# Low part of the keys on 128 rows instead of 64 in the selected and sliding scores

## The chip, the cores and the metric

One core of one Trainium2 chip runs the whole program. The metric is the device time of one execution in microseconds (us); the median of the runs shown is what counts. The engines are PE (matmul; PEld is its weight load), DVE (vector), ACT (scalar), POOL (GpSimd) and SP (which issues most transfers).

## What is computed

The reference runs a first transformer block with two layers, then a second block. The change lies in the first block's attention, called NSA: 512 tokens, 8 query heads in 2 groups of 4 that share keys and values of 64 channels. Three softmax branches are gated and summed: over compressed keys, over selected key blocks and over a sliding window.

```python
n_slc = T // SLC_BLOCK              # 512 // 64 = 8
top_n = min(SLC_TOPK, n_slc)        # min(16, 8) = 8: every block is selected
...
sc = jnp.einsum('bqhgd,bhqnld->bhgqnl', qc, kg).astype(jnp.float32) * scale
...
sc = jnp.einsum('bqhgd,bkhd->bhgqk', qb, kb).astype(jnp.float32) * scale   # sliding, window 512
p = jax.nn.softmax(jnp.where(mask, sc, NEG_INF), axis=-1)
...
o = g[..., 0:1] * o_cmp + g[..., 1:2] * o_slc + g[..., 2:3] * o_win
```

With 512 tokens, both the selected and the sliding branch are plain causal attention, each with its own keys and values.

## The kernel before

**Products in parts.** A float32 value is held as a high part rounded to the matmul's format (`fp32r`) and a low part, the rest. A gemm takes three passes (high by high, high by low, low by high; lines 223 to 225).

**Where the parts of queries and keys lie.** A head has 64 channels, PE has 128 rows. `qS` holds a head's query with its high part in one half of the rows and its low part in the other; for heads of group 0 the high part is in rows 0 to 63, for group 1 in rows 64 to 127. `khh[kv]` holds the keys' high part of group kv in both halves, for both branches (b = 0 selected, b = 1 sliding). One pass of 128 rows by `khh` so sums two products. The keys' low part lies in `kl`, group 0 in rows 0 to 63 and group 1 in rows 64 to 127; the pass by `kl` takes the 64 rows in which the query's high part is.

**Building the keys.** `nsa_in` projects keys, values and queries. During its last gemm (`gemm_V(512, post_sv, ...)`, the values of another attention) it runs side jobs between weight units. `tr_k(i)` transposes the keys of token tile i (128 tokens): ACT copies the high parts to `khh` (line 901) and half of the compression's input to `KT2` (in `tA`, line 902), DVE subtracts for `kl` (line 905) and copies the other half of `KT2` (line 906). After all four tiles, POOL adds a table to `KT2` (`blocks`, line 929, first for `blk[0]`, then for `blk[1]`), and PE multiplies the sums by the compression's weights (line 938).

**The heads.** `nsa_attn` goes over 32 items per layer: 4 query tiles of 128 rows (i = 0 to 3), 8 heads each. Item t is a pipeline: `s0(t)` scores and exponentials, `s1(t)` scaling, `s2(t)` transposes, `s3(t)` the product with the values, on successive turns of the loop; PE's order is that of the code. For i = 0 the scores of both branches (2 x 128 columns) are one pass by `khh` (line 1084), one by `kl` (line 1085) and two mask passes (line 1087). For i of 1 to 3 each branch has L = 256, 384 or 512 columns, and per branch there is one pass by `khh` (line 1079), one by `kl` (line 1080) and one mask pass of 128 columns with bf16 operands (line 1081). DVE takes the maximum (line 1090), ACT the exponentials (line 1092) into one of four buffers `E[t % 4]`: two of their own, and the gain tiles `gpost` and `gpre`.

**Filling.** Between the steps, `fill` runs pieces of other gemms ("units" of 24 passes of 512 columns, lines 223 to 225). In the heads the units have one PSUM bank, number 7: a unit's first pass waits until ACT has copied the unit before it out. `cmp_turn` (line 1066) uses that bank too.

The borrowed weight slots `K4` hold the key tiles, so profile and order call `khh[0]`, `khh[1]` and `kl` by the slots' names: in the first layer `whi_72`, `wlo_73` and `whi_70`.

Of the kernel before, what the change touches and what calls it, by code (L numbers as in the profile page):

```python
# [8 lines left out]
F32 = mybir.dt.float32  # L9
F32R = mybir.dt.float32r  # L10
# [6 lines left out]
T = 512  # L17
# [156 lines left out]
class Net:  # L174
# [633 lines left out]
    def mix1(self, l):  # L808
        tc = self.tc
        pool = lambda st, name, side: st.enter_context(tc.tile_pool(name=name, bufs=1, side=side))  # L810
        with ExitStack() as st:
            O = pool(st, "oA", "left")
            oA = (O.tile([128, 4, T], F32R, name="oAh"), O.tile([128, 4, T], F32R, name="oAl"))
            tA = O.tile([128, 8, T], F32, name="tA")
            with ExitStack() as sb:
                S = pool(sb, "sv", "right")
                sv = S.tile([128, 4, 512], F32, name="sv")
                with ExitStack() as sn:
                    NP = pool(sn, "nsa", "left")
                    qS = NP.tile([128, 8, T], F32R, name="qS")  # L820
                    vN = NP.tile([128, 4, 2, 128], F32, name="vN")
                    vc = NP.tile([128, 2, 4, 64], F32, name="vc")
                    gt = NP.tile([128, 4, 24], F32, name="gt")
                    gcm = NP.tile([128, 4, 8], F32, name="gcm")
                    with ExitStack() as s2:
                        K4 = self.nsa_in(l, pool(s2, "nsain", "left"), qS, vN, vc, gt, gcm, sv, tA)
                    S = pool(sb, "sqk", "right")
                    sq = S.tile([128, 4, T], F32, name="sq")
                    sk = S.tile([128, 4, T], F32, name="sk")
                    with ExitStack() as s2:  # L830
                        self.nsa_attn(pool(s2, "nsaat", "left"), qS, K4, vN, vc, gt, gcm, oA, sq, sk, tA)
                O = pool(st, "oB", "left")
                oB = (O.tile([128, 4, T], F32R, name="oBh"), O.tile([128, 4, T], F32R, name="oBl"))
                with ExitStack() as s2:
                    self.sb_attn(pool(s2, "sbat", "left"), sq, sk, sv, oB, self.merge_a(oA, tA))
            self.merge_out(st, 4, oB, tA, self.a["g_post_mix"][l], self.a["g_pre_ffn"][l])

    def nsa_in(self, l, R, qS, vN, vc, gt, gcm, sv, tA):
        nc, a = self.nc, self.a
        if not self.begin:  # L840
            self.banks, self.bi = list(range(8)), 0
# [2 lines left out]
        t1 = [self.gpost.rearrange("p (e h s d) -> p e h s d", e=2, h=8, s=2)[:, e] for e in range(2)]  # L844
        t2 = [R.tile([128, 8, 2, 32], F32, name=f"t2_{i}") for i in range(2)]
        KT2 = tA[:, 0:2].rearrange("p a (k n) -> p a k n", k=2)
        blk = [R.tile([128, 16, 2, 31], F32, name="blk"),
               self.gpre[:, 0:992].rearrange("p (l k n) -> p l k n", l=16, k=2)]
        w1 = [R.tile([128, 16, 64], F32, name=f"w1_{i}") for i in range(2)]
        w2 = R.tile([128, 64], F32, name="w2")  # L850
# [3 lines left out]
        half = [slice(0, 64), slice(64, 128)]  # L854
# [37 lines left out]
        def tr_k(i):  # L892
            ps = side_bank()
            v = ps.rearrange("p (k t) -> p k t", k=4)
            for k in range(4):
                nc.tensor.transpose(v[:, k], kr[i][:, k], self.ident)
            tok = slice(i * 128, i * 128 + 128)
            old = [v[h].rearrange("p k (u e) -> p k u e", e=2) for h in half]
            for kv in range(2):
                for h in half:  # L900
                    nc.scalar.activation(khh[kv][h, :, tok], v[half[kv], 2:4], AF.Copy)
                nc.scalar.activation(KT2[half[0], :, kv, i * 64:i * 64 + 64], old[kv][:, 0:2, :, 0], AF.Copy)
            for kv in range(2):
                h = half[kv]
                nc.vector.tensor_sub(kl[h, :, tok], v[h, 2:4], khh[kv][h, :, tok].bitcast(F32))
                nc.vector.tensor_copy(KT2[half[1], :, kv, i * 64:i * 64 + 64], old[kv][:, 0:2, :, 1])

        def tr_q(i):
# [75 lines left out]
        self.gemm_V(280, post_win)  # L984
        K4 = self.W.borrow()
        khh = [t.rearrange("p (b n) -> p b n", b=2) for t in K4[0:2]]
        kl = K4[2].rearrange("p (b n) -> p b n", b=2)
        kc = K4[3][:, 0:896].rearrange("p (c k n) -> p c k n", c=2, k=2)
        nc.vector.memset(kc.bitcast(F32), 0.0)
        gates()  # L990
# [6 lines left out]
            seq(compressed, lambda: tr_q(3))])  # L997
        return K4

    def nsa_attn(self, R, qS, K4, vN, vc, gt, gcm, oA, sq, sk, tA):  # L1000
        nc, PS = self.nc, self.PS
        mm = nc.tensor.matmul
        E = [R.tile([128, 2, T], F32, name=f"E{i}") for i in range(2)]
        E += [t.rearrange("p (b n) -> p b n", b=2) for t in (self.gpost, self.gpre)]
        PT = [h.rearrange("p (b j q) -> p b j q", b=2, j=4)[:, b] for h in self.hn for b in range(2)]
        Ec = tA[:, 6:8].rearrange("p a (i h n) -> p (a i) h n", i=2, h=8)
        khh = [t.rearrange("p (b n) -> p b n", b=2) for t in K4[0:2]]
        kl = K4[2].rearrange("p (b n) -> p b n", b=2)
        kc = K4[3][:, 0:896].rearrange("p (c k n) -> p c k n", c=2, k=2)
        PcT = R.tile([128, 4, 2, 128], F32, name="PcT")  # L1010
        self.banks = [7]
# [9 lines left out]
        sums = [None] * 4  # L1021
# [3 lines left out]
        n = len(items)  # L1025
        Ob = PS[:, 6, :]

        def cmp_scores():
            raw = [E[3].rearrange("p b n -> p (b n)")[:, kv * T:kv * T + T] for kv in range(2)]
            for kv in range(2):  # L1030
                for c in range(2):
                    for g in range(4):
                        mm(PS[:, 4 + kv, :], kc[:, c, kv, 96 - 32 * g:224 - 32 * g], qS[:, 4 * kv + g],
                           start=c + g == 0, stop=c + g == 4)
                if kv:
                    nc.vector.tensor_copy(raw[kv], PS[:, 4 + kv, :])
                else:
                    nc.scalar.activation(raw[kv], PS[:, 4 + kv, :], AF.Copy)
            for kv in range(2):
                ps = PS[:, 4 + kv, :].rearrange("p (i n) -> p i n", i=4)  # L1040
                for i in range(4):
                    nc.tensor.transpose(ps[:, i], raw[kv][:, i * 128:i * 128 + 128], self.ident)
                nc.vector.tensor_add(Ec[:, :, 4 * kv:4 * kv + 4], ps.rearrange("p i (g n) -> p i g n", g=4),
                                     self.cmask[:, :, None, :].to_broadcast([128, 4, 4, 32]))
# [25 lines left out]
        def s0(t):  # L1070
            i, h = items[t]
            kv, g = divmod(h, 4)
            L = (i + 1) * 128
            r = slice(64 * kv, 64 * kv + 64)
            q = qS[:, h, i * 128:L]
            if i:
                S2 = PS[:, 2 * (t % 2):2 * (t % 2) + 2, :L]
                for b in range(2):
                    mm(S2[:, b], q, khh[kv][:, b, :L], start=True, stop=False)
                    mm(S2[:, b], q[r], kl[r, b, :L], start=False, stop=False)  # L1080
                    mm(S2[:, b, i * 128:L], self.identb, self.maskb, start=False, stop=True)  # L1081
            else:
                S2 = PS[:, 2 * (t % 2), 0:256].rearrange("p (b n) -> p b n", b=2)
                mm(S2, q, khh[kv][:, :, :L], start=True, stop=False)
                mm(S2, q[r], kl[r, :, :L], start=False, stop=False)
                for b in range(2):
                    mm(S2[:, b], self.identb, self.maskb, start=False, stop=b == 1)
            e = E[t % 4]
            m, sums[t % 4] = self.sm(2), self.sm(2)
            nc.vector.reduce_max(m, S2, axis=AX.X, negate=True)  # L1090
            for b in range(2):
                nc.scalar.activation(e[:, b, :L], S2[:, b], AF.Exp, bias=m[:, b:b + 1], accum_out=sums[t % 4][:, b:b + 1])

        def s1(t):
            i, h = items[t]
            L = (i + 1) * 128
            e, s = E[t % 4], sums[t % 4]
            nc.vector.reciprocal(s, s)
            nc.vector.tensor_mul(s, s, gt[:, i, h * 3 + 1:h * 3 + 3])
            for b in range(2):  # L1100
                nc.vector.tensor_scalar(e[:, b, :L], e[:, b, :L], s[:, b:b + 1], None, op0=OP.mult)

        def s2(t):
            i, h = items[t]
            e = E[t % 4]
            for b in range(2):
                tb = PS[:, 4 + b, :].rearrange("p (j q) -> p j q", j=4)
                for j in range(i + 1):
                    nc.tensor.transpose(tb[:, j], e[:, b, j * 128:j * 128 + 128], self.ident)  # L1109
                p = PT[2 * (t % 2) + b]  # L1110
                if b:
                    nc.vector.tensor_copy(p[:, :i + 1], tb[:, :i + 1])
                else:
                    nc.scalar.activation(p[:, :i + 1], tb[:, :i + 1], AF.Copy)
# [610 lines left out]
```

## Time and profile before

| | us |
|---|---|
| median of 3 runs (2938.53 to 2940.01) | 2939.97 |
| the profiled execution's own time | 2941.05 |
| its span | 2939.1 |
| PE busy | 2885.7 (98%) |
| DVE busy | 1402.1 (48%) |
| ACT busy | 1130.7 (38%) |
| POOL busy | 369.1 (13%) |

PE is busy nearly throughout, but a matmul's end in the trace is modelled, so a busy PE does not say how fast it goes. What a pass costs is read from the distance between the starts of successive passes. The first layer's heads run from about 110 to 290 us of the span, the second layer's from about 963 to 1143 us.

### The profile page before, as it was taken

Reading aid. Unit: us, or ns where it says so; the run is one execution under the profiler, and the core shown is the slowest. Engines: PE = TensorE matmul, PEld = TensorE weight load, DVE = VectorE, ACT = ScalarE, POOL = GpSimd, SP = SyncE. Lnnn points to the kernel's source line nnn. Section 1 sums busy time; section 2 is a strip of 40 time slices with the busy share of each in tenths; the row PEclk is TensorE's granted clock in tenths of the full one; section 3 lists DMA queues with packets and bytes.
Section 4 is the critical chain, followed back from the end, with each engine's and each line's share of the span. In section 5 each row is a group of like instructions: output and inputs, shape, how many; then the busy total and the mean of one; then the engine's idle time right before and its main releaser. Section 6 shows DMA issues by size and latency. Waiting matters only on the chain.

```text
span 2939.1 us, 34966 instructions
## 1 busy us (share of the span) xinstructions
PE 2885.7 (98%) x14228; PEld 2302.4 (78%) x14228; DVE 1402.1 (48%) x2232; ACT 1130.7 (38%) x2046; POOL 369.1 (13%) x287
## 2 busy tenths in 40 slices
PE   8999999999999999999999999999999999999999
PEld 7777578888878776688888888888776978888887
DVE  4655645544555555555535453233653243533333
ACT  3444644433433445634424342222443232432222
POOL 5221100100122111100101020000522010000000
PEclk9999999999999999999999999999999999999999
DMA  4111023333322111132332323322421222322322
GB/s 157 58 57 30 23 94 111 99 115 96 102 97 88 48 47 32 49 131 72 111 109 91 109 89 97 99 95 95 137 84 52 72 68 98 115 90 89 109 87 79
DMA packets 234322, 255.48 MB, mean 87 GB/s; under 512 B 33073, under 2 KB 193185, under 8 KB 233777
## 3 DMA queue, kind: packets, MB, share of 16 engines
q1 hardware_dynamic: 228016, 233.53, 25.0%
q0 software_dynamic: 4992, 16.94, 1.7%
q10 hardware_dynamic: 1152, 2.77, 0.3%
q8 instruction: 111, 1.82, 0.2%
q14 instruction: 51, 0.41, 0.0%
HBM read 248.60 MB, written 5.53 MB: 86 GB/s over the span
## 4 chain that ended last, share of the span: by engine, by line
PE 91%; DVE 5%; ACT 3%; issue 1%; DMA 0%; DVEq 0%; SPq 0%; ACTq 0%
PE PS L223 25%; PE PS L225 24%; PE PS L224 24%; PE PS L422 2%; PE PS L1189 2%; DVE x L585 1%; PE PS L1123 1%; PE PS L1109 1%; PE PS L1080 1%; PE PS L1484 1%; PE PS L425 1%; PE PS L1223 1%; PE PS L460 1%; PE PS L1213 1%; PE PS L1215 1%
## 5 line engine op out<-in xcount | busy, mean ns | idle before, releaser
L121 DVE TENSOR_TENSOR wlo<-wraw,whi 128x1024 fp32r<-128x1024 f32 (+3 forms) x364 | 437.3, 1206 | 729.2 <-ACT whi L112 729.1
L223 PE MATMUL PS<-Hh,whi 128*128 128x512 f32 x1952 | 777.3, 398 | 1.0 <-ACT PcT L1067 0.6
L225 PE MATMUL PS<-Hh,wlo 128*128 128x512 f32 x1952 | 761.2, 390 | 0.2 <-DVE wlo L121 0.2
L224 PE MATMUL PS<-Hl,whi 128*128 128x512 f32 x1952 | 760.5, 390 | 0.0
L112 ACT ACTIVATE whi<-wraw 128x1024 fp32r<-128x1024 f32 (+2 forms) x432 | 436.8, 1016 | 342.1 <-PE PS L225 286.2
L223 PEld LDWEIGHTS PS<-Hh,whi 128*128 128x128 f32 x1952 | 367.0, 188 | 87.6 <-issue 14.5
L225 PEld LDWEIGHTS PS<-Hh,wlo 128*128 128x128 f32 x1952 | 366.4, 188 | 78.3 <-DVE wlo L121 0.9
L224 PEld LDWEIGHTS PS<-Hl,whi 128*128 128x128 f32 x1952 | 367.0, 188 | 70.1
L121 POOL TENSOR_TENSOR wlo<-wraw,whi 128x1024 fp32r<-128x1024 f32 (+1 forms) x68 | 167.2, 2460 | 1339.1 <-ACT whi L112 1339.1
L223 PE MATMUL PS<-whi,gh 128*128 128x512 f32 x624 | 242.7, 389 | 0.0
L225 PE MATMUL PS<-whi,gl 128*128 128x512 f32 x624 | 242.7, 389 | 0.0
L224 PE MATMUL PS<-wlo,gh 128*128 128x512 f32 x624 | 242.7, 389 | 0.0
L231 ACT ACTIVATE gh<-gg 128x512 fp32r<-128x512 f32 x88 | 55.6, 632 | 327.2 <-DVE gg L643 178.9
L223 PEld LDWEIGHTS PS<-whi,gh 128*128 128x128 f32 x624 | 117.1, 188 | 24.5
L224 PEld LDWEIGHTS PS<-wlo,gh 128*128 128x128 f32 x624 | 117.1, 188 | 24.4
L225 PEld LDWEIGHTS PS<-whi,gl 128*128 128x128 f32 x624 | 117.1, 188 | 24.1
L641 POOL TENSOR_TENSOR gg<-cg,cu 128x512 f32<-128x512 f32 x44 | 56.7, 1289 | 549.4 <-DVE cu L624 549.4
L223 PE MATMUL PS<-whi,Hh 128*128 128x512 f32 (+2 forms) x320 | 118.8, 371 | 2.2 <-ACT whi L112 1.9
L232 DVE TENSOR_TENSOR gl<-gg,gh 128x512 fp32r<-128x512 f32 x88 | 60.9, 692 | 125.7 <-ACT gh L231 125.7
L224 PE MATMUL PS<-wlo,Hh 128*128 128x512 f32 (+2 forms) x320 | 116.8, 365 | 0.5 <-DVE wlo L121 0.5
L225 PE MATMUL PS<-whi,Hl 128*128 128x512 f32 (+2 forms) x320 | 116.3, 363 | 0.4 <-DVE Hl L232 0.4
L1090 DVE TENSOR_REDUCE small<-PS 128x2 f32<-128x256 f32 (+3 forms) x64 | 52.7, 824 | 106.0 <-PE PS L1081 95.0
(341 smaller groups left out, 4140.0 us busy)
## 6 DMA issues: line engine op xcount, KB each, us to landing
wraw<-in_w_in_dram SPq DMA_DIRECT2D x56, 1024.0 KB, 5.0
wraw<-in_w_up_dram SPq DMA_DIRECT2D x40, 1024.0 KB, 5.1
wraw<-in_ffn_w_gate_dram SPq DMA_DIRECT2D x20, 1024.0 KB, 5.2
wraw<-in_ffn_w_up_dram SPq DMA_DIRECT2D x20, 1024.0 KB, 5.2
wraw<-in_w_down_dram SPq DMA_DIRECT2D x16, 1024.0 KB, 5.0
wraw<-in_ffn_w_down_dram SPq DMA_DIRECT2D x16, 1024.0 KB, 5.0
wraw<-in_w_out_dram SPq DMA_DIRECT2D x12, 1024.0 KB, 5.0
wraw<-in_w_down_dram SPq DMA_DIRECT2D x8, 768.0 KB, 4.3
```

Of the source, the lines that this page charges most:

```text
L112: self.nc.scalar.activation(hi, raw, AF.Copy)
L121: self.lo.tensor_sub(lo, raw, hi.bitcast(F32))
L223: mm(out, lh, rh, start=start, stop=False)
L224: mm(out, lh, rl, start=False, stop=False)
L225: mm(out, ll, rh, start=False, stop=stop)
L231: nc.scalar.activation(hi, src, AF.Copy)
L232: nc.vector.tensor_sub(lo, src, hi.bitcast(F32))
L422: self.nc.tensor.matmul(ps[:, sl], ww[:, k], self.Hh[:, k, sl], start=k == 0 and ww is w[0], stop=False)
L425: self.nc.tensor.matmul(ps[:, sl], w[0][:, kk], self.Hl[:, kk, sl], start=False, stop=kk == 7)
L641: nc.gpsimd.tensor_mul(g, cg[j % 3], cu[j % 3])
L1090: nc.vector.reduce_max(m, S2, axis=AX.X, negate=True)
L1189: mm(z, sk[r, p, j * 128:j * 128 + 128], sq[r, p, j * 128:], start=True, stop=False)
```

## The change

There is a second tile for the keys' low part, `kl1`, so that `kll[0]` and `kll[1]` hold the low part of group 0 and 1 in both halves of the rows. The pass by the low part then takes all 128 rows of `qS`, which adds the product of the two low parts. In blocks of i from 1 to 3 the masks of both branches come after the four score passes. `tr_k` subtracts twice per group instead of once. For the room, the exponentials use three buffers instead of four (`E[t % 3]`), the compressed scores are copied through `PcT` instead of `E[3]`, and `blk[0]` lies in `tA[:, 2:4]`, which is free at that time.

```diff
+                    kl1 = NP.tile([128, 1024], F32R, name="kl1")
...
-        blk = [R.tile([128, 16, 2, 31], F32, name="blk"),
+        blk = [tA[:, 2:4].rearrange("p a n -> p (a n)")[:, 0:992].rearrange("p (l k n) -> p l k n", l=16, k=2),
...
             for kv in range(2):
-                h = half[kv]
-                nc.vector.tensor_sub(kl[h, :, tok], v[h, 2:4], khh[kv][h, :, tok].bitcast(F32))
+                for h in half:
+                    nc.vector.tensor_sub(kll[kv][h, :, tok], v[half[kv], 2:4], khh[kv][half[kv], :, tok].bitcast(F32))
...
+        kll = [t.rearrange("p (b n) -> p b n", b=2) for t in (K4[2], kl1)]
...
-        E = [R.tile([128, 2, T], F32, name=f"E{i}") for i in range(2)]
+        E = [R.tile([128, 2, T], F32, name="E0")]
...
-            raw = [E[3].rearrange("p b n -> p (b n)")[:, kv * T:kv * T + T] for kv in range(2)]
+            raw = [PcT.rearrange("p i k q -> p (i k q)")[:, kv * T:kv * T + T] for kv in range(2)]
...
-            r = slice(64 * kv, 64 * kv + 64)
...
                 for b in range(2):
-                    mm(S2[:, b], q, khh[kv][:, b, :L], start=True, stop=False)
-                    mm(S2[:, b], q[r], kl[r, b, :L], start=False, stop=False)
+                    for k in (khh[kv], kll[kv]):
+                        mm(S2[:, b], q, k[:, b, :L], start=k is khh[kv], stop=False)
+                for b in range(2):
                     mm(S2[:, b, i * 128:L], self.identb, self.maskb, start=False, stop=True)
...
-                mm(S2, q, khh[kv][:, :, :L], start=True, stop=False)
-                mm(S2, q[r], kl[r, :, :L], start=False, stop=False)
+                for k in (khh[kv], kll[kv]):
+                    mm(S2, q, k[:, :, :L], start=k is khh[kv], stop=False)
...
-            e = E[t % 4]
+            e = E[t % 3]
```

On PE, a block of i = 1 in the first layer between two fill units, before (`identb` and `maskb` are the mask's operands):

```order
L225 MATMUL PS<-Hh,wlo_67 128x512
L1079 MATMUL PS<-wlo_73,qS 128x256
L1080 MATMUL PS<-whi_70,qS 128x256
L1081 LDWEIGHTS identb
L1081 MATMUL PS<-maskb,identb 128x128
L1079 MATMUL PS<-wlo_73,qS 128x256
L1080 MATMUL PS<-whi_70,qS 128x256
L1081 LDWEIGHTS identb
L1081 MATMUL PS<-maskb,identb 128x128
L223 MATMUL PS<-Hh,whi_66 128x512
```

and now (`kl_154` is the new tile):

```order
L225 MATMUL PS<-Hh,wlo_67 128x512
L1080 MATMUL PS<-wlo_73,qS 128x256
L1080 MATMUL PS<-kl_154,qS 128x256
L1080 MATMUL PS<-wlo_73,qS 128x256
L1080 MATMUL PS<-kl_154,qS 128x256
L1082 LDWEIGHTS identb
L1082 MATMUL PS<-maskb,identb 128x128
L1082 LDWEIGHTS identb
L1082 MATMUL PS<-maskb,identb 128x128
L223 MATMUL PS<-Hh,whi_66 128x512
```

The eight passes stay eight; the first mask pass has moved behind the second branch's score passes, and the passes by the low part name another tile.

On DVE, the last token tile of `tr_k` in the first layer and the row after it, before:

```order
L905 TENSOR_TENSOR whi_70<-PS,whi_72 64x2x128
L906 COPY tA<-PS 64x2x64
L905 TENSOR_TENSOR whi_70<-PS,wlo_73 64x2x128
L906 COPY tA<-PS 64x2x64
L121 TENSOR_TENSOR wlo_69<-wraw_65,whi_68 128x1024
```

and now:

```order
L906 TENSOR_TENSOR whi_70<-PS,whi_72 64x2x128 x2
L907 COPY tA<-PS 64x2x64
L906 TENSOR_TENSOR kl_154<-PS,wlo_73 64x2x128 x2
L907 COPY tA<-PS 64x2x64
L121 TENSOR_TENSOR wlo_69<-wraw_65,whi_68 128x1024
```

Each group's one subtraction has become two, so the last copy to `tA` (which is `KT2`) stands behind two more instructions of its tile. PE, DVE and ACT otherwise keep their order in these places; POOL and SP keep theirs throughout.

## Rows read from the trace of the kernel before

**Rows 1.** The page: chain that ended last, share of the span by engine.

```profile
PE 91%; DVE 5%; ACT 3%; issue 1%; DMA 0%; DVEq 0%; SPq 0%; ACTq 0%
```

**Rows 2.** Busy time of engines in one stretch of the heads (PE, PEld, DVE, ACT, POOL).

```profile
148.00:190.00 42.00, 41.28 (x242) 30.48 (x241) 22.11 (x52) 17.42 (x56) 9.63 (x4) 1.00 0.16 51
```

**Rows 3.** Waits of PE, first layer's heads: total, times, longest.

```profile
PE PS L1066 <- ACT PcT L1067: 0.4, 1, 0.4
PE PS L1123 <- ACT hn L1114: 0.4, 1, 0.4
PE PS L1084 <- DVE qS L918: 0.2, 1, 0.2
```

**Rows 4.** Timeline of PE, a block of 256 columns: start, duration, engine, line.

```profile
155.72 0.28 PE L1079 MATMUL PS<-wlo,qS 128*128 128x256 f32 x1
155.92 0.38 PE L1080 MATMUL PS<-whi,qS 64*128 64x256 f32 x1
156.24 0.23 PE L1081 MATMUL PS<-maskb,identb 128*128 128x128 bf16 x1
156.27 0.36 PE L1079 MATMUL PS<-wlo,qS 128*128 128x256 f32 x1
156.57 0.38 PE L1080 MATMUL PS<-whi,qS 64*128 64x256 f32 x1
156.88 0.23 PE L1081 MATMUL PS<-maskb,identb 128*128 128x128 bf16 x1
156.92 0.47 PE L223 MATMUL PS<-Hh,whi 128*128 128x512 f32 x1
```

**Rows 5.** Timeline of PE: ten passes of 512 columns, then a 512-column block.

```profile
278.10 0.40 PE L225 MATMUL PS<-Hh,wlo 128*128 128x512 f32 x1
...
280.16 0.39 PE L225 MATMUL PS<-Hh,wlo 128*128 128x512 f32 x1
280.39 0.39 PE L1079 MATMUL PS<-wlo,qS 128*128 128x512 f32 x1
...
282.04 0.47 PE L223 MATMUL PS<-Hh,whi 128*128 128x512 f32 x1
```

**Rows 6.** Timeline of PE: seventeen passes of 280 columns, first and last.

```profile
74.23 0.29 PE L223 MATMUL PS<-whi,Hh 128*128 128x280 f32 x1
...
76.28 0.29 PE L224 MATMUL PS<-wlo,Hh 128*128 128x280 f32 x1
```

**Rows 7.** Timeline of PE, a block of the first query tile.

```profile
115.80 0.38 PE L1085 MATMUL PS<-whi,qS 64*128 64x256 f32 x1
116.12 0.28 PE L1087 MATMUL PS<-maskb,identb 128*128 128x128 bf16 x2
116.21 0.47 PE L223 MATMUL PS<-Hh,whi 128*128 128x512 f32 x1
```

**Rows 8.** Timelines of ACT and PE at one fill unit's end.

```profile
158.79 0.59 ACT L1015 ACTIVATE sq<-PS 128x512 f32<-128x512 f32 x1
159.81 0.48 PE L223 MATMUL PS<-Hh,whi 128*128 128x512 f32 x1
```

**Rows 9.** Timeline of DVE: last token tile of the key transposes.

```profile
92.20 0.42 DVE L905 TENSOR_TENSOR whi<-PS,whi 64x256 fp32r<-64x256 f32 x1 [0.78 <-ACT tA L902]
...
93.28 0.29 DVE L906 COPY tA<-PS 64x128 f32<-64x128 f32 x1
```

**Rows 10.** Timeline of POOL: the first add ahead of the compression.

```profile
93.70 3.43 POOL L929 TENSOR_TENSOR blk<-tA,pe 128x992 f32<-128x992 f32 x1 [14.98 <-ACT whi L112]
```

**Rows 11.** Waits of PE in the gemm ahead of the heads.

```profile
PE PS L938 <- POOL gpre L929: 2.0, 1, 2.0
PE PS L938 <- POOL blk L929: 1.1, 1, 1.1
```

**Rows 12.** Stretches after those waits, two layers: busy times, PEclk, DMA share, GB/s.

```profile
101.00:104.00 3.00, 3.00 (x31) 2.69 (x28) 0.00 (x0) 1.65 (x3) 0.00 (x0) 0.50 0.00 0
951.00:957.00 6.00, 5.36 (x68) 5.07 (x69) 1.67 (x1) 1.62 (x3) 0.59 (x1) 0.50 0.05 16
```

More of the change, by code (lines that the diff above doesn't have):

```diff
@@ L824, in mix1 @@
                     gcm = NP.tile([128, 4, 8], F32, name="gcm")
+                    kl1 = NP.tile([128, 1024], F32R, name="kl1")
                     with ExitStack() as s2:
-                        K4 = self.nsa_in(l, pool(s2, "nsain", "left"), qS, vN, vc, gt, gcm, sv, tA)
+                        K4 = self.nsa_in(l, pool(s2, "nsain", "left"), qS, vN, vc, gt, gcm, kl1, sv, tA)
                     S = pool(sb, "sqk", "right")
@@ L830, in mix1 @@
                     with ExitStack() as s2:
-                        self.nsa_attn(pool(s2, "nsaat", "left"), qS, K4, vN, vc, gt, gcm, oA, sq, sk, tA)
+                        self.nsa_attn(pool(s2, "nsaat", "left"), qS, K4, vN, vc, gt, gcm, kl1, oA, sq, sk, tA)
                 O = pool(st, "oB", "left")
@@ L836, in mix1, with nsa_in @@
             self.merge_out(st, 4, oB, tA, self.a["g_post_mix"][l], self.a["g_pre_ffn"][l])
-    def nsa_in(self, l, R, qS, vN, vc, gt, gcm, sv, tA):
+    def nsa_in(self, l, R, qS, vN, vc, gt, gcm, kl1, sv, tA):
         nc, a = self.nc, self.a
@@ L986, in nsa_in @@
         khh = [t.rearrange("p (b n) -> p b n", b=2) for t in K4[0:2]]
-        kl = K4[2].rearrange("p (b n) -> p b n", b=2)
+        kll = [t.rearrange("p (b n) -> p b n", b=2) for t in (K4[2], kl1)]
         kc = K4[3][:, 0:896].rearrange("p (c k n) -> p c k n", c=2, k=2)
@@ L998, in nsa_in, with nsa_attn @@
         return K4
-    def nsa_attn(self, R, qS, K4, vN, vc, gt, gcm, oA, sq, sk, tA):
+    def nsa_attn(self, R, qS, K4, vN, vc, gt, gcm, kl1, oA, sq, sk, tA):
         nc, PS = self.nc, self.PS
         mm = nc.tensor.matmul
-        E = [R.tile([128, 2, T], F32, name=f"E{i}") for i in range(2)]
+        E = [R.tile([128, 2, T], F32, name="E0")]
         E += [t.rearrange("p (b n) -> p b n", b=2) for t in (self.gpost, self.gpre)]
@@ L1007, in nsa_attn @@
         khh = [t.rearrange("p (b n) -> p b n", b=2) for t in K4[0:2]]
-        kl = K4[2].rearrange("p (b n) -> p b n", b=2)
+        kll = [t.rearrange("p (b n) -> p b n", b=2) for t in (K4[2], kl1)]
         kc = K4[3][:, 0:896].rearrange("p (c k n) -> p c k n", c=2, k=2)
@@ L1096, in s1 @@
             L = (i + 1) * 128
-            e, s = E[t % 4], sums[t % 4]
+            e, s = E[t % 3], sums[t % 4]
             nc.vector.reciprocal(s, s)
@@ L1104, in s2 @@
             i, h = items[t]
-            e = E[t % 4]
+            e = E[t % 3]
             for b in range(2):
```

## The prediction

> **What bounds the kernel now.** I read the chain that ended last first: 91% of it is PE [rows 1]. In the heads, where the scores are, a stretch of 42 us shows PE busy for 41.28, DVE for 22.11 and ACT for 17.42 [rows 2]. The list of PE's waits over the first layer's heads holds five entries, 1.7 us in all, of which three matter here [rows 3]. So a pass that PE gets through sooner moves the end, unless one of those few waits, or a new one, swallows it. A "busy" PE hides the price of a pass, since matmul ends are modelled. The timeline of starts shows it, and there the passes on 64 rows stand out.
>
> **What the 64-row passes cost.** Take a block of 256 columns [rows 4]. From the pass by `khh` to the pass by `kl` it takes 0.20 us (155.72 to 155.92), from there to the mask 0.32, to the next `khh` pass 0.03, then 0.30, 0.31 and 0.04: 1.20 us from the first pass to the next gemm's first. Passes that stay on 128 rows go far quicker: ten of 512 columns have nine distances in 2.06 us, 0.229 each [rows 5], and seventeen of 280 columns have sixteen in 2.05 us, 0.128 each [rows 6]. Every one of these has its own weight load. The slope between them, 0.101 us over 232 columns, gives 0.118 us for 256 columns and 0.173 for 384, an estimate by that line. Each step onto and off 64 rows therefore adds about 0.08 and 0.20 us to what the columns take: PE evidently doesn't hide the new weights behind the running pass when the number of rows changes, and the way back costs more.
>
> **The change, part by part.**
>
> *Blocks of i = 1 to 3.* Now: four passes on 128 rows at the steady distance and two masks. Two masks in a row up to the next pass are seen in a block of the first tile: 116.12 to 116.21, 0.09 us [rows 7]. So 256 columns take 4 x 0.118 + 0.09 = 0.56 us instead of 1.20, saving 0.64. A 512-column block takes 1.65 us now (280.39 to 282.04) [rows 5] and then 4 x 0.229 + 0.09 = 1.01, saving 0.64. For 384 columns the middle of 1.20 and 1.65 is 1.43, against 4 x 0.173 + 0.09 = 0.78: again 0.64. With 8 heads, 3 tiles and 2 layers there are 48 blocks: 30.7 us.
>
> *Blocks of i = 0.* The step from `khh` to the low part goes from 0.20 (taken from [rows 4], same shape) to 0.118, that from the low part to the mask from 0.32 (115.80 to 116.12) [rows 7] to 0.118: 0.28 us each, 16 blocks, 4.5 us. Gross, that is 35.2 us.
>
> *What waits give back in the heads, per layer.* In i = 0 I count five of eight blocks as lost. After block 0 the next block waits for DVE's part of the queries (0.2 us, line 1084), and after block 4 the value product waits for an ACT copy (0.4 us, line 1123) [rows 3]; both ends hang on other engines. After blocks 3, 5 and 7 PE needs bank 7, and ACT's copy ends only 0.05 to 0.07 us before PE takes the bank. That is 5 x 0.28 = 1.4 us. The first block of i = 1 runs ahead of the second `cmp_turn`, which waits for `PcT` (0.4 us) [rows 3]; only the 0.28 us by which block 7 lets that copy start sooner remain, so 0.36 is lost. In i = 1 to 3 the bank is handed over at 11 unit ends. At the tightest one, ACT's copy runs 158.79 to 159.38 and PE takes the bank at 159.81 [rows 8], 0.43 us later; less 0.05 for the signal, 0.38 of that block's 0.64 are free and 0.26 are lost. Five others have 0.64 or 0.65 us and lose about 0.04 each, the remaining five have 0.69 to 3.7 and lose nothing: 0.45 us with the first. Sum 2.2 us, for two layers 4.4. Net 30.8 us.
>
> *Building the second low part.* DVE does four more instructions per group and layer, 0.42 us each. A token tile takes DVE 1.37 us now (92.20 to 93.28 + 0.29), after 0.78 us of waiting for ACT [rows 9]: ACT sets a period of 2.15 us. With two more subtractions DVE needs 1.37 + 0.84 = 2.21. The idle time covers the first three tiles but for 0.06 each; the last copy to `KT2` comes 0.84 + 3 x 0.06, about 1.0 us later. Behind it stand POOL's add, which starts at 93.70, just after DVE's last copy (93.57) [rows 10], and PE, which already waits 1.1 and 2.0 us for POOL there [rows 11]. So this lands on PE in full: 1.0 us a layer, 2.0 us. Without a delay of DVE it would be nothing; that bounds it below. Above, PE's idle time there is followed by a low clock: 3 us at granted clock 0.50 in the first layer, 6 in the second (1.2 GHz instead of 2.4) [rows 12]. If a longer idle time brings 3 us more of it per layer, half of that is lost, 3 us for both; if less, up to 1.5 us per layer come back.
>
> *Three buffers instead of four, `PcT` for the raw scores, `blk[0]` in `tA`.* Nothing. Item t takes the buffer of t-3, whose transposes stand ahead of `s0(t)` in PE's own order, and the exponential waits for that block's scores anyhow. `PcT` is written by `cmp_turn` only after six items; the gate units write `tA[:, 2:4]` long after the compression. The cover would be gone only if an exponential could precede its scores.
>
> *Sum.* 30.8 - 2.0 = 28.8 us. The profiled execution took 2941.05 us (span 2939.1), so 2912.2 for one like it; it lies 1.1 above the median of 2939.97, and from that I forecast 2911.2 us.
>
> **A rule that speaks against it.** The distances on 128 rows leave hardly any room for an exposed weight load: 0.128 us for 280 columns [rows 6]. The Trainium skill, TensorE: Matmul & The Clock Gate, Part 3 (What overlaps and what doesn't), says that a weight load overlaps a running matmul only where the row groups differ. By that, two passes on the same 128 rows should expose it, and this trace disagrees. The sum by that rule stands among the rivals.
>
> **The rivals.**
>
> *The way back belongs to the mask.* In this block the 0.20 us between the low part and the mask follow a change of rows and also one of format, fp32r to bf16; no row shows the second alone. If the format is the cause, one of two stays per block: 0.64 - 0.20 = 0.44 for 48 blocks, 21.1 us, and 0.08 for 16, 1.3 us; less waits (0.8 us a layer, the bank being hardly touched) and 2.0 for DVE: 18.8 us, so 2921.2. For it: nothing but that both coincide; against it, the change onto 64 rows costs without a change of format.
>
> *Weight loads stay exposed.* The first step's 0.20 us (0.31 at 512 columns by the slope) then holds for all four passes: 4 x 0.20 + 0.09 = 0.89 and 4 x 0.31 + 0.09 = 1.33, saving 0.31 and 0.32; 48 blocks 15.1 us, 16 of 0.12 us 1.9, less 1.6 and 2.0: 13.4 us, so 2926.6. Against it [rows 5, 6].
>
> *Bank 7 takes it.* Were each of the 22 handovers in i = 1 to 3 to cost a whole block's saving, 14.1 us would go, of which 0.9 are counted: 2924.4. Against it is the room measured at the other handovers.
>
> *It doesn't do what it says.* If the slow steps came from loading the same query tile twice, they would stay, and only DVE's 2.0 us be added: 2942. Against it: gemm passes too repeat their weights (lines 223 and 224 in a fill unit differ only in one operand) at 0.229.
>
> *Slower.* PE's longer idle time ahead of the compression keeps the clock at 0.50 [rows 12] beyond the few us seen. It decides from 29 us of PE work per layer at that clock (half of 58 is the whole gain), and past 0.2% slower from 35. Lasting through the first two query tiles, some 80 us a layer, it would cost 40 each: 2991. For it only that the second layer shows twice the first's low stretch; against it, PE is dense after it and the clock comes back within 7 us in both.
>
> **How the numbers follow.** My forecast 0.76, the mask 0.12, exposed loads 0.05, bank 7 0.03, no effect 0.02, slower 0.02. The likeliest gives 2911.2. Downwards, the bound is that nothing is given back and DVE's part is hidden: 2939.97 - 35.2 = 2904.8, and 1.5 for a shorter low clock: 2903. Upwards the range takes in the mask's case, 2921.5, which leaves about 0.12 out. 0.2%, 5.9 us, is about what a measurement of this kernel can tell from no change. Faster by more: 0.96, the first four cases; within: 0.02; slower: 0.02.
>
> **What would show it.** In the changed profile, the distances inside a 256-column block should be 0.12, 0.12, 0.12, 0.12 and 0.09; a distance of 0.3 ahead of the first mask shows the mask's case, 0.20 between score passes exposed loads. PE's waits should show bank 7 (line 223 for ACT `sq`, `sk` or `tA`) with a few tenths, and line 939 for POOL with 1.0 us more in each layer. The heads of each layer should be shorter by 15.4 us, and nothing else should move. The forecast is wrong if the blocks shrink but the heads don't, or if PEclk stays at 0.5 for long after the compression.

## The result and the profile after

The changed kernel takes 2909.62 us (median of 4 runs, 2909.34 to 2910.56); the kernel before, run beside it, 2939.25 (4 runs, 2937.72 to 2940.01). The ratio is 0.99, with a 95% interval of 0.9887 to 0.9912: 29.6 us less. The forecast was 2911.2 in a range of 2903.0 to 2921.5. The profiled execution after took 2909.57 us with a span of 2907.6, against 2939.1 before: 31.5 us less. (The profiled execution of before lay 1.8 above the median measured beside the change; that is the difference between 31.5 and 29.6.)

On the page of after, PE's busy time has gone from 2885.7 to 2852.1 us, 33.6 less, and DVE's has risen by 16.3. The chain that ended last is still PE's (compare [rows 1]):

```profile
PE 2852.1 (98%) x14228; PEld 2301.0 (79%) x14228; DVE 1418.4 (49%) x2248; ACT 1130.1 (39%) x2046; POOL 370.0 (13%) x287
...
PE 92%; DVE 4%; ACT 2%; issue 1%; DMA 0%; DVEq 0%; ACTq 0%; POOL 0%; POOLq 0%
```

**The block.** PE's timeline of after, the same 256-column block as in [rows 4]; columns are start, duration, engine, line, operands:

```profile
155.46 0.28 PE L1080 MATMUL PS<-wlo,qS 128*128 128x256 f32 x1
155.57 0.28 PE L1080 MATMUL PS<-kl,qS 128*128 128x256 f32 x1
155.69 0.28 PE L1080 MATMUL PS<-wlo,qS 128*128 128x256 f32 x1
155.81 0.28 PE L1080 MATMUL PS<-kl,qS 128*128 128x256 f32 x1
155.93 0.29 PE L1082 MATMUL PS<-maskb,identb 128*128 128x128 bf16 x2
156.03 0.48 PE L223 MATMUL PS<-Hh,whi 128*128 128x512 f32 x1
```

The distances between starts are 0.11, 0.12, 0.12, 0.12 and, for the two masks, 0.10: 0.57 us, where it was 1.20. At 512 columns the block takes 1.01 us (255.33 to 256.34), where it was 1.65 [rows 5].

**The waits.** PE's waits in the first layer's heads after (engine and line, releaser, total, times, longest):

```profile
PE PS L1067 <- ACT PcT L1068: 1.0, 1, 1.0
PE PS L1043 <- DVE PcT L1037: 0.4, 1, 0.4
PE PS L1110 <- ACT hn L1115: 0.3, 1, 0.3
PE PS L1086 <- DVE qS L919: 0.2, 1, 0.2
```

Against [rows 3]: the second `cmp_turn` now waits 1.0 instead of 0.4, and the wait of the value product for ACT's `hn` (line 1123 before, 1124 now) is gone. Ahead of the heads the two waits for POOL are 1.6 and 2.0, where [rows 11] has 1.1 and 2.0:

```profile
PE PS L939 <- POOL gpre L930: 2.0, 1, 2.0
PE PS L939 <- POOL tA L930: 1.6, 1, 1.6
```

**Where the time came from**, by the starts of the same steps in both traces:

| step | forecast, us | measured, first / second layer |
|---|---|---|
| up to the key transposes (`tr_k`) | 0 | +0.50 / +0.24 |
| `tr_k` to the first compression matmul | +1.0 | +0.78 / +0.78 |
| compression to the first scores | 0 | +0.97 / -1.04 |
| heads | -15.4 | -16.48 / -16.51 |
| of which i = 0 | -0.84 | -1.96 in the first layer |
| of which i = 1 to 3 | -14.55 | -4.56, -4.82, -5.13 = -14.52 (rounded) in the first layer |
| behind the second layer's heads | 0 | -0.74 |

The forecast's shares of the heads follow from its own terms: 8 x 0.28 - 1.4 for i = 0, and 24 x 0.64 - 0.36 - 0.45 for the rest.

### The profile page after: what moved, and what is told of

Read it like the earlier page. It is cut to its first block, busy times and chain, and to the rows that moved or that the text cites. A ratio compares the mean times of both kernels' runs of the same rounds, so it can differ in the third digit from the quotient of the medians.

```text
span 2907.6 us, 34978 instructions
## 1 busy us (share of the span) xinstructions
PE 2852.1 (98%) x14228; PEld 2301.0 (79%) x14228; DVE 1418.4 (49%) x2248; ACT 1130.1 (39%) x2046; POOL 370.0 (13%) x287
## 4 chain that ended last, share of the span: by engine, by line
PE 92%; DVE 4%; ACT 2%; issue 1%; DMA 0%; DVEq 0%; ACTq 0%; POOL 0%; POOLq 0%
PE PS L223 26%; PE PS L225 25%; PE PS L224 25%; PE PS L422 2%; PE PS L1190 2%; DVE x L585 1%; PE PS L1124 1%; PE PS L1110 1%; PE PS L1485 1%; PE PS L1080 1%; PE PS L425 1%; PE PS L460 1%; PE PS L1224 1%; PE PS L1214 1%; PE PS L1216 1%; DVE hn L339 1%
```

## The experiments

The theory: changing the number of rows between passes costs time on PE, about 0.08 us on and 0.20 off, whatever the formats; filling the rows removes it. Rivals: the cost belongs to the mask's format, to the 64-row pass itself, or to another part of the change (its order, its three buffers). A second question came from the waits for POOL: what the second low part costs, and whether that can be had back. Lines in the rows are those of each experiment's own file.

**Rows alone.** The changed kernel with everything as changed (two tiles, masks last, three buffers), but the low pass on 64 rows:

```diff
-                    for k in (khh[kv], kll[kv]):
-                        mm(S2[:, b], q, k[:, b, :L], start=k is khh[kv], stop=False)
+                    mm(S2[:, b], q, khh[kv][:, b, :L], start=True, stop=False)
+                    mm(S2[:, b], q[r], kll[kv][r, b, :L], start=False, stop=False)
...
-                for k in (khh[kv], kll[kv]):
-                    mm(S2, q, k[:, :, :L], start=k is khh[kv], stop=False)
+                mm(S2, q, khh[kv][:, :, :L], start=True, stop=False)
+                mm(S2, q[r], kll[kv][r, :, :L], start=False, stop=False)
```

> The changed kernel with one thing undone: the pass by the low part takes 64 rows again (second tile, masks at the end, three buffers all stay). Theory, that the change of the number of rows is what costs: a 256-column block takes 0.20 + 0.31 + 0.20 + 0.31 + 0.09 = 1.1 us or more again, of which the 0.31 from a 64-row pass to the next khh pass has no change of format, so the way back costs without the mask; time 2937 to 2942 us. Rival, that the masks' place or the buffers brought the gain: 2910 to 2925 us.

2944.52 us (10 runs) against 2940.34 for before beside it (13 runs): ratio 1.0014, interval 1.0004 to 1.0023. The whole gain is gone. PE's timeline of this kernel, a block of 256 columns:

```profile
156.54 0.28 PE L1080 MATMUL PS<-wlo,qS 128*128 128x256 f32 x1
156.75 0.38 PE L1081 MATMUL PS<-kl,qS 64*128 64x256 f32 x1
157.06 0.39 PE L1080 MATMUL PS<-wlo,qS 128*128 128x256 f32 x1
157.38 0.38 PE L1081 MATMUL PS<-kl,qS 64*128 64x256 f32 x1
157.69 0.28 PE L1083 MATMUL PS<-maskb,identb 128*128 128x128 bf16 x2
157.78 0.47 PE L223 MATMUL PS<-Hh,whi 128*128 128x512 f32 x1
```

The third row is the one to read: 156.75 to 157.06 is 0.31 us from 64 rows to 128 with no mask and no change of format. In the changed kernel the step from the low part to the mask, with a change of format and of weights (from the query tile to `identb`) and without one of rows, takes 0.12. So the 0.20 us belong to the rows, and the mask's rival falls, and with it the thought that new weights cost as such. That the kernel lies 2.5 us above the highest time expected is the rest of the change without its gain: a block takes 1.24 us instead of 1.20, the heads are 0.99 and 0.95 us longer than before, the added subtractions cost some 0.8 per layer, together 3.5 of the 4.2 us.

**Grouped passes.** Before, with nothing but the order changed: both high passes, both low ones on 64 rows, both masks.

```diff
                 for b in range(2):
                     mm(S2[:, b], q, khh[kv][:, b, :L], start=True, stop=False)
+                for b in range(2):
                     mm(S2[:, b], q[r], kl[r, b, :L], start=False, stop=False)
+                for b in range(2):
                     mm(S2[:, b, i * 128:L], self.identb, self.maskb, start=False, stop=True)
```

> The kernel before with the passes of a block in another order: khh, khh, low, low (on 64 rows as before), mask, mask; no second tile. Theory, that each CHANGE of the number of rows costs: 256 columns take 0.12 + 0.20 + 0.12 + 0.31 + 0.09 = 0.84 instead of 1.20 us, 48 blocks save 17 us, less about 2 for waits: 2922 to 2927 us. Rival, that each PASS on 64 rows is slow in itself: the distance between the two low passes is 0.2 to 0.3 us, a block about 1.0, time 2930 to 2935 us.

2924.25 us (4 runs), ratio 0.9947, interval 0.9932 to 0.9961: 16.1 us less, with the same passes on the same rows. Timeline of PE (x2 is two passes in one row):

```profile
153.40 0.40 PE L1079 MATMUL PS<-wlo,qS 128*128 128x256 f32 x2
153.73 0.50 PE L1081 MATMUL PS<-whi,qS 64*128 64x256 f32 x2
154.16 0.28 PE L1083 MATMUL PS<-maskb,identb 128*128 128x128 bf16 x2
154.25 0.47 PE L223 MATMUL PS<-Hh,whi 128*128 128x512 f32 x1
```

From the first low pass to the mask it takes 0.43 us, which is one steady distance of 0.12 and one way back of 0.31. A 64-row pass behind another costs what a 128-row pass does; the change of rows is what costs. The block takes 0.85 us. One change in and out per block instead of two is worth 0.35 of the 0.64, and 48 x 0.35 = 16.8 is what came: the heads are 8.43 and 8.44 us shorter in the two layers.

**Three buffers alone.** Before with `E[t % 3]`, `raw` in `PcT` and one `E` tile less:

```diff
-        E = [R.tile([128, 2, T], F32, name=f"E{i}") for i in range(2)]
+        E = [R.tile([128, 2, T], F32, name="E0")]
...
-            e = E[t % 4]
+            e = E[t % 3]
```

> The kernel before with three exponential buffers instead of four and the compressed scores copied through PcT, nothing else. Theory, that these cost nothing because PE's own order already keeps a buffer free: the distances and PE's waits in the heads are those of before, and the time is that of before within 2 us. Rival, that a buffer less holds up an exponential and so a later step: waits of ACT on PE's transposes and a longer stretch of heads, 2942 us or more.

2940.27 us (10 runs) against 2940.39 (19 runs): ratio 0.9998, interval 0.9988 to 1.0007. The heads agree with before within 0.03 us. Nothing, as the prediction had it. (The place of `blk[0]` was not tried by itself.)

**The wait that vanished.** In i = 0 the gain was 1.1 us larger than forecast, all of it between the fifth block and the sixth. PE's timeline of before there shows the product with the values standing for 1.41 us (135.19 to 136.60); in the changed kernel the same eight matmuls take 0.59. Before:

```profile
135.19 0.43 PE L1123 MATMUL PS<-hn,vN 128*64 128x128 f32 x2
136.01 0.65 PE L1123 MATMUL PS<-hn,vN 128*64 128x128 f32 x6 [0.39 <-ACT hn L1114]
136.60 0.44 PE L1109 MATMUL PS<-cf,gpost 128*128 128x128 f32 x2
```

And after:

```profile
136.58 0.66 PE L1124 MATMUL PS<-hn,vN 128*64 128x128 f32 x8
137.17 0.44 PE L1110 MATMUL PS<-cf,gpre 128*128 128x128 f32 x2
```

ACT's copy `hn` was late because ACT waited 2.97 us for DVE's addition to the compressed scores. Timeline of ACT, then those of DVE and POOL, before:

```profile
134.74 1.06 ACT L1052 ACTIVATE tA<-tA 128x1024 f32<-128x1024 f32 x1 [2.97 <-DVE tA L1051]
135.70 0.26 ACT L1114 ACTIVATE hn<-PS 128x128 f32<-128x128 f32 x1
```

```profile
131.29 3.41 DVE L1051 TENSOR_TENSOR tA<-tA,small 128x1024 f32<-128x1024 f32 x1
...
131.14 2.48 POOL L121 TENSOR_TENSOR wlo<-wraw,whi 128x1024 fp32r<-128x1024 f32 x1 [9.24 <-ACT whi L112]
```

And after:

```profile
132.66 1.22 DVE L1052 TENSOR_TENSOR tA<-tA,small 128x1024 f32<-128x1024 f32 x1
...
132.80 3.34 POOL L121 TENSOR_TENSOR wlo<-wraw,whi 128x1024 fp32r<-128x1024 f32 x1 [8.94 <-ACT whi L112]
```

Before, POOL's subtraction began 0.15 us ahead of DVE's addition, and DVE took 3.41 us; now DVE begins 0.14 us ahead, takes 1.22, and POOL takes 3.34 instead of 2.48. Whoever comes second ends about its own time after the other (DVE 1.08 us behind POOL's end, POOL 2.26 behind DVE's). The Trainium skill, SBUF — State Buffer (SBUF: two separate sides), says that a GpSimd operation and a DVE operation with two inputs in SBUF take turns at a shared pair of ports, whole instruction by whole instruction; these rows agree.

Every trace of this case has it the same way, in both layers: the addition takes 3.41 or 3.42 us in the five kernels with the low part on 64 rows and POOL at work (before, rows alone, grouped, three buffers, before with the copies first), and 1.22 in the changed kernel and all variants of it on 128 rows. As the rows-alone kernel, which has the rest of the change, keeps 3.42, it is the low pass on 128 rows that turned the meeting. In the changed kernel the next DVE operation of this size meets POOL instead (3.39 us, 0.08 behind POOL's start), but no wait of PE is listed for it.

To test that the wait hangs on this meeting, before had its low parts in the heads made on DVE, so that POOL is not there at all:

```diff
-        self.W.defer, self.W.lo = True, nc.gpsimd
+        self.W.defer = True
```

> The kernel before, the low parts of the fill units' weights in the heads made by DVE instead of POOL. Theory, that the wait of the value product for ACT's copy (0.4 us, line 1123, the fifth item) comes from a DVE addition that takes 3.41 us beside a POOL subtraction instead of 1.2: that addition takes 1.2 us, the wait goes, and the stretch from the first to the ninth item is shorter by up to 0.8 us in each layer. Rival, that the wait has another source: it stays at 0.4 us.

One run, 2944.42 us. DVE's addition in it:

```profile
132.97 1.22 DVE L1051 TENSOR_TENSOR tA<-tA,small 128x1024 f32<-128x1024 f32 x1
```

The wait for `hn` is gone from the list of PE's waits, and the stretch up to the sixth block is shorter by 0.42 and 0.49 us in the two layers, about half of the 0.8 hoped for. The addition is short again but begins 1.68 us later, behind DVE's own subtraction; so it ends 0.51 sooner, `hn` starts 0.52 sooner (135.18), and the product takes 0.98 us (135.10 to 136.08). The heads as a whole are 2.87 and 1.25 us slower, for DVE now has POOL's work: in the first layer PE waits 1.3 us for ACT's `PcT` copy later on. That POOL's subtraction stretches the addition, and that the wait hangs on the addition's end, is shown; the full 0.8 us is not reproduced by this edit.

**What the second low part costs.** Five kernels reorder DVE's (and ACT's) work of `tr_k`, so that the copies to `KT2`, for which POOL and then PE wait, come sooner. The plainest, from the changed kernel, puts both copies of a tile ahead of its four subtractions:

```diff
             for kv in range(2):
+                nc.vector.tensor_copy(KT2[half[1], :, kv, i * 64:i * 64 + 64], old[kv][:, 0:2, :, 1])
+            for kv in range(2):
                 for h in half:
                     nc.vector.tensor_sub(kll[kv][h, :, tok], v[half[kv], 2:4], khh[kv][half[kv], :, tok].bitcast(F32))
-                nc.vector.tensor_copy(KT2[half[1], :, kv, i * 64:i * 64 + 64], old[kv][:, 0:2, :, 1])
```

> The changed kernel, DVE's two copies to KT2 put ahead of its four subtractions within each token tile. Theory, that the added subtractions delay POOL's add by way of the last copy: PE's first wait for POOL ahead of the compression goes from 1.6 to 0.6 us or less in each layer, 2906 to 2909 us. Rival, that the longer wait came from something else (POOL, ACT): both waits stay at 1.6 and 2.0 us and the time at 2909.6.

2903.51 us (4 runs), ratio 0.9876, interval 0.9859 to 0.9892: 2.5 us below the least expected. PE's waits ahead of the heads:

```profile
PE PS L940 <- POOL gpre L931: 2.5, 1, 2.5
PE PS L914 <- DVE kl L908: 0.4, 1, 0.4
```

2.9 us instead of 3.6. That alone is 1.4 us over two layers. The rest is clock, from the windows (length, busy times, then PEclk). After, first layer, then second:

```profile
100.80:102.00 1.20, 1.20 (x24) 1.20 (x26) 0.99 (x1) 0.00 (x0) 0.00 (x0) 0.50 0.01 2
102.00:106.00 4.00, 4.00 (x50) 3.79 (x49) 0.00 (x0) 1.51 (x2) 0.00 (x0) 0.50 0.01 4
...
938.50:940.00 1.50, 1.50 (x40) 1.50 (x42) 0.98 (x1) 0.00 (x0) 0.00 (x0) 0.74 0.00 1
940.00:943.00 3.00, 3.00 (x35) 2.81 (x32) 0.00 (x0) 1.44 (x2) 0.00 (x0) 0.56 0.00 0
```

With the copies first:

```profile
97.00:100.00 3.00, 0.51 (x13) 0.37 (x13) 2.91 (x5) 2.34 (x2) 2.61 (x1) 1.00 0.46 118
100.00:104.00 4.00, 4.00 (x70) 3.60 (x67) 1.48 (x2) 2.19 (x3) 0.00 (x0) 1.00 0.51 178
...
934.00:940.00 6.00, 6.00 (x46) 5.08 (x42) 1.75 (x3) 2.78 (x4) 0.00 (x0) 1.00 0.12 42
```

After loses half of 5.2 us in the first layer, 2.6, and 0.26 x 1.5 + 0.44 x 3 = 1.7 in the second; here PE comes out of its idle time at the full 2.4 GHz. 1.4 and 4.3 make 5.7 of the 6.1 us between the two medians; by the starts, from `tr_k` to the first scores, it is 3.3 and 2.3 us in the two layers.

The same kernel was run once more, on another chip, beside the changed one, also run again.

> The changed kernel as it is, timed beside the next one on the same chip: 2908 to 2912 us.

> The changed kernel with DVE's copies first in each token tile, as run before (2903.5 us), now beside the changed kernel: 2902 to 2906 us, and its profile shows again no fall of the clock in the first layer. Rival, that the gain over the changed kernel beyond about 2 us was the chance of where the low clock fell: 2906 to 2909 us.

The changed kernel: 2909.39 us, ratio 0.9891, interval 0.9874 to 0.9907. The copies first: 2907.5 (2902.09, 2907.11, 2907.9 and 2909.41), ratio 0.9883, interval 0.9868 to 0.9898, which misses what was expected and lies in the rival's range. But the rival's place is not the right one: the waits are the same to a tenth, and PEclk is 1.00 at this place again in its profiled run of 2907.11. That run and the first one's profiled run (2904.24) keep step within 0.4 us at each step of the table above, up to the end of the second layer's heads; in the 12 us behind them the second loses 3.0 us, at granted clock 0.50 (1.2 GHz). The same window in the first run, then in the second:

```profile
1112.00:1118.00 6.00, 6.00 (x29) 3.50 (x28) 4.01 (x11) 3.77 (x10) 0.00 (x0) 1.00 0.00 0
...
1112.00:1118.00 6.00, 6.00 (x18) 3.50 (x17) 2.77 (x8) 3.37 (x9) 0.00 (x0) 0.50 0.00 0
```

The kernel is the same, and so is the idle time of 0.84 us just ahead in both. Of the 6.1 us by which this order beat the changed kernel at first, 1.9 are left beside it; what the copies first are worth for certain is the shorter waits.

The mirror of it in the kernel before (both copies ahead of the two subtractions):

> The kernel before, DVE's two copies to KT2 ahead of its two subtractions in each token tile. Theory, that most of what this order brought the changed kernel is PE's wait ahead of the compression and the low clock behind it, which stand in the kernel before too: the waits of 1.1 and 2.0 us shrink by about 0.4, and 0 to 2 us per layer of low clock go: 2935 to 2939 us. Rival, that it only repairs what the added subtractions cost: the time of before within 1 us.

2936.91 us (10 runs), ratio 0.9991, interval 0.9981 to 1.0, in the range expected, though the interval reaches 1: PE's waits for POOL fall from 1.1 and 2.0 to one of 2.4. From `tr_k` to the first scores it takes 0.71 and 1.69 us less in the two layers; the clock fell in both all the same (mean PEclk 0.76 from 99 to 106 us and from 949 to 956). The start of the first layer's heads moved by -0.01 us and that of the second by -3.13, but +0.70 and -1.46 of that came ahead of `tr_k`, where nothing was changed.

Moving the subtractions further back was tried in two ways. First, all copies of the four tiles ahead of all high parts and subtractions, which stand in `tr_k2`:

```diff
-            seq(*[lambda i=i: tr_k(i) for i in range(4)]),
+            seq(*[lambda i=i: tr_k(i) for i in range(4)], *[lambda i=i: tr_k2(i) for i in range(4)]),
...
```

> The changed kernel, all copies to KT2 (ACT's and DVE's, four token tiles) ahead of all high parts and subtractions. Theory, that PE's waits of 1.6 and 2.0 us ahead of the compression hang on the time of the last copy alone: POOL's adds end before PE comes to them, both waits go, 3.6 us a layer, and the low clock behind them shrinks (up to 2 us a layer): 2898 to 2903 us. Rival, that the high and low parts, now later, hold up the weights' low parts or the first scores: waits on lines 224 or of the first score pass appear, 2906 to 2910 us.

2908.72 us (4 runs), ratio 0.9894, interval 0.9879 to 0.9908. The rival came true. POOL starts at 89.56 instead of 95.03, PE no longer waits for it, but the PSUM banks of the key transposes are read out later, and the query transposes need them:

```profile
PE PS L919 <- DVE kl L913: 3.2, 2, 2.2
```

Second, ACT's and DVE's copies first in each tile, and the subtractions one tile later:

```diff
+                nc.vector.tensor_copy(KT2[half[1], :, kv, i * 64:i * 64 + 64], old[kv][:, 0:2, :, 1])
...
+            for i2 in ([i - 1] if i else []) + ([i] if i == 3 else []):
+                tok2 = slice(i2 * 128, i2 * 128 + 128)
...
+                        nc.vector.tensor_sub(kll[kv][h, :, tok2], trk[i2][half[kv], 2:4], khh[kv][half[kv], :, tok2].bitcast(F32))
```

> The changed kernel, the copies to KT2 of a token tile ahead of its high parts on ACT, and on DVE ahead of the subtractions of the tile before. Theory: POOL's first add starts about 2.7 us sooner than with the copies first in each tile on DVE alone, PE's wait of 2.5 us ahead of the compression falls below 0.6 in each layer, the clock does not fall there, and no long wait for the transposes' banks appears: 2897 to 2901 us. Rival, that PE then waits for those banks as it did with all copies first: 2904 to 2909 us.

2905.7 us (4 runs), ratio 0.9883, interval 0.9869 to 0.9898: the rival again, in the first layer 3.1 us of waits at the query transposes. DVE's timeline shows what was not foreseen, that each of DVE's copies waits for ACT's copy of the same group:

```profile
88.64 0.28 DVE L904 COPY tA<-PS 64x128 f32<-64x128 f32 x1 [1.92 <-ACT tA L903]
89.26 0.29 DVE L904 COPY tA<-PS 64x128 f32<-64x128 f32 x1 [0.34 <-ACT tA L903]
```

POOL's first add so started at 95.29, no sooner than in the changed kernel.

From the two misses: copies first in each tile, and only tile 2's subtractions put off, behind tile 3's copies.

```diff
...
-                for h in half:
-                    nc.vector.tensor_sub(kll[kv][h, :, tok], v[half[kv], 2:4], khh[kv][half[kv], :, tok].bitcast(F32))
                 nc.vector.tensor_copy(KT2[half[1], :, kv, i * 64:i * 64 + 64], old[kv][:, 0:2, :, 1])
+            trk[i] = v
+            for i2 in ((0,), (1,), (), (2, 3))[i]:
+                tok2 = slice(i2 * 128, i2 * 128 + 128)
+                for kv in range(2):
+                    for h in half:
+                        nc.vector.tensor_sub(kll[kv][h, :, tok2], trk[i2][half[kv], 2:4], khh[kv][half[kv], :, tok2].bitcast(F32))
```

> The changed kernel, DVE's copies to KT2 ahead of the subtractions in each token tile, and the subtractions of tile 2 behind the copies of tile 3. Theory: the last copy comes about 1.3 us sooner than with the copies first in each tile, only tiles 0 and 1 hold banks that the next transposes need and their subtractions are not moved, so PE's wait for POOL falls from 2.5 to about 1.2 us in each layer: 2900 to 2902 us. Rival, that the rest of the wait hangs on something else (ACT's copies, POOL itself): 2903 to 2905 us.

2900.5 us (4 runs) against 2941.16 for before beside it: ratio 0.9863, interval 0.9849 to 0.9878, the best of all kernels here. PE's waits, ahead of the first layer's heads:

```profile
PE PS L945 <- POOL gpre L936: 0.9, 1, 0.9
PE PS L919 <- DVE kl L913: 0.4, 1, 0.4
```

1.3 us instead of 3.6, twice 2.3 = 4.6; and PEclk is 1.00 here in both layers, worth the 4.3 above. Together 8.9 us, which is the difference to the changed kernel run beside it (2909.39). That it agrees to the tenth is luck: the 4.3 are the losses of the first run's trace, and the run beside lost 1.0 more in the second layer.

A part of the shorter wait is the meeting of DVE and POOL again. In the changed kernel POOL's first add begins 0.10 us behind a DVE subtraction (line 121, 94.93) and takes 3.37; here POOL comes first, its adds take 2.52 and 2.45, and the subtraction takes 2.57 instead of 1.23:

```profile
94.89 2.45 POOL L936 TENSOR_TENSOR gpre<-tA,pe 128x992 f32<-128x992 f32 x1
...
95.85 2.57 DVE L121 TENSOR_TENSOR wlo<-wraw,whi 128x1024 fp32r<-128x1024 f32 x1
```

## Why the prediction was right, step by step

- **Price of a change of rows.** Right, and shown from both sides: filling the rows takes it away (0.57 us a block), keeping 64 rows in the changed kernel brings it back (1.24 us), and grouping saves half. The saving of 0.64 per block comes out at 0.62 to 0.66 where nothing waits, at all three lengths. The estimated distances on the line between 280 and 512 columns were right to 0.01. Why a change of rows costs is not shown. The prediction puts it down to weights that are not loaded behind the running pass; in before's list of weight loads the load for the 64-row pass does start only with the pass (155.92), but so does the mask's in the changed kernel (155.93), where the step takes 0.12.
- **Blocks of i = 0: the term that was mis-sized.** The step "after block 4 the value product waits for an ACT copy ... both ends hang on other engines" counted that block's 0.28 us as lost, on the ground that the wait's length was fixed by ACT. It was set by a meeting of DVE and POOL, of which the prediction says nothing, and a shift of 0.3 us between them (DVE's addition 1.37 us later, POOL's subtraction 1.66) turned who came first. The block kept its 0.28 and the product got through 0.82 sooner, 1.1 us a layer, 2.2 us in all. The 0.39 us in the list of waits understated this, since it counts from the modelled end of the second matmul; the starts show the product at 1.41 us instead of 0.59. Blocks 0, 3, 5 and 7 lost theirs as forecast, the step from block 7 to the next being unchanged to 0.00.
- **Bank 7.** Right in kind, and in sum by luck. For i = 1 to 3 the bank was to take 0.45 us and the first block to lose 0.36. The bank took some 0.7: five unit ends lost 0.05 to 0.11 each rather than about 0.04, the tightest 0.30 rather than 0.26. There PE now takes the bank 0.05 us after ACT's copy, as timelines of ACT and PE after show at one of them (compare [rows 8]):

```profile
194.78 0.60 ACT L718 ACTIVATE tA<-PS 128x512 f32<-128x512 f32 x1
...
195.43 0.50 PE L223 MATMUL PS<-Hh,whi 128*128 128x512 f32 x1
```

  These waits stand in no list, since PE's modelled ends cover them. Against it stands the first block's step, which kept 0.55 us of its 0.64 where 0.28 were granted: the two misses of 0.27 cancel. The second `cmp_turn` does wait 0.6 us longer (1.0, not 0.4), but line 223, which waited 0.3 us for the same copy, no longer does.
- **The second low part.** 0.78 us a layer, forecast 1.0; the chain is as forecast. The last copy ends at 94.90 and POOL's add starts at 95.03, where it was 93.57 and 93.70 [rows 9, 10]; of these 1.33 us, 0.50 were there before `tr_k`. DVE's token tile takes 2.16 us (86.27 to 88.43) rather than the 2.21 of the forecast, so the 0.06 per tile hardly came. Experiments with the copies first have this cost back and more.
- **Low clock.** The bounds held. With the longer idle time came 5.2 us at 1.2 GHz in the first layer where [rows 12] has 3, and a shorter low stretch in the second; the two nearly cancel (+0.97, -1.04). That the idle time decides it is not shown: the changed kernel's second run has +0.98 and -0.01. The slower rival has nothing for it: from 106 us on PEclk is 0.97.
- **Buffers.** Nothing, shown by themselves but for the place of `blk[0]`.
- **The rivals.** The mask and the doubled query tile fall to the 64-row experiment (0.31 us without a format change, from the very tile that gives 0.12 with 128 rows); exposed weight loads fall to the 0.12 of the block after; bank 7 took tenths.

The sum by what was measured: 2 x 16.5 = 33.0 us of heads, less 1.6 for the low part, 31.4 of the span's 31.5. The other rows of the table nearly cancel: 0.74 lost ahead of `tr_k` and 0.74 won behind the second layer's heads, where the change alters no step, and 0.07 won between compression and scores. Against the 31.5 of the profiled pair the forecast of 28.8 was 2.7 short, 2.2 by the meeting and 0.45 by the low part; by the medians, 29.6 apart, it looks nearer than its terms were.

## What to carry to other kernels

Look at PE's starts, not at its busy time: a lone 64-row pass among 128-row passes cost 0.3 us here, and it goes away by filling the rows with something useful or harmless, or half of it by putting the passes of equal rows next to each other, which needs no memory at all. When an edit adds work to an engine, put what another engine waits for ahead of the addition within the same step, but don't hold PSUM banks that the next step needs: two attempts that did moved the wait to the next user of the bank, and the one that put off only a tile whose bank was not needed soon did not. Before a short wait is booked as fixed, see what sets its other end; a shift of 0.3 us turned a meeting of two engines here.

## What was not expected of the hardware

A DVE addition of 128 x 1024 float32 took 1.22 us alone and 3.41 when it began 0.15 us behind a POOL subtraction; with the order reversed, the subtraction went from 2.48 to 3.34 us. The clock after the idle time ahead of the compression is not settled by the work alone: the grouped kernel and the one with three buffers, which don't touch the steps ahead of the heads, show PEclk 1.00 from 101 to 104 us where before shows 0.50 [rows 12], after the same two waits of 1.1 and 2.0 us [rows 11]. The window of the grouped kernel:

```profile
101.00:104.00 3.00, 3.00 (x17) 2.52 (x16) 0.00 (x0) 2.78 (x4) 0.00 (x0) 1.00 0.00 0
```

By the starts that is 1.5 us from compression to scores in the first layer; in the second both fall to 0.50 as before does. Two runs of one kernel differ as much: the changed kernel by 1.0 us in the second layer, the copies first by 3.0 behind the second layer's heads. So comparisons of two kernels here hold 1 to 3 us that the edit may have nothing to do with, and part of what the reordered kernels differ by may be that; what decides it stays open.
